# Second half of a layer norm started by single tiles, three projections in turn, and fill-in work ordered behind the chain's copies, in a hybrid RWKV-7 / short-convolution trunk layer

## The chip, the cores and the metric

The kernel runs on one core of one Trainium2 chip. The metric is the device time of one execution in microseconds (us). TensorE (PE) multiplies matrices, VectorE (DVE), ScalarE (ACT) and GpSimd (POOL) work on tiles of 128 partitions, and SyncE (SP) issues most of the DMAs. Each of the engines has its own instruction stream and works through it in order, so an instruction that waits holds up all that stand behind it on its engine.

## What is computed

One layer over 544 tokens of width 1024 (512 of a prompt, and 8 requests of 4 tokens each):

```
x    = layer_norm(ALPHA*x + 0.5*swiglu(x, ffn1), ln1)
proj = x @ w_in
r,k,v,wd,ad,gd = token-shifted mix of the first 1792 columns of proj
decay = f(w0 + tanh(wd) @ w_lora_up);  a = sigmoid(a0 + ad @ a_lora_up);  g = sigmoid(gd) @ g_lora_up
kk   = k*k_k, normalized by head;   k = k*(1 + (a-1)*k_a)
S_t  = S diag(decay) + (S (-kk)) (kk*a)^T + v k^T;   o_t = S_t r          # 8 heads of 64
y_rwkv = (group_norm(o) + sum(r*k*r_k)*v) * g
u    = c_c * c_h;   y_conv = c_b * (3-tap causal convolution of u)       # 512 channels
x    = layer_norm(ALPHA*x + [y_rwkv, y_conv] @ w_out, ln2)
x    = layer_norm(ALPHA*x + 0.5*swiglu(x, ffn2), ln3)
```

The new states (recurrence, shift, convolution) are outputs too. All numbers are fp32.

## The kernel before

**Layout.** Activations lie transposed, channels on partitions, tokens along the free axis, in two halves of the tokens (`HALF`: 256 of the prompt, then 256 and the 32 of the requests). An fp32 product is made of three matmuls: each operand is split into a high part (a copy on ACT, rounded to the type that PE multiplies) and a low part (the difference, on DVE). `mm3` issues hi·hi, hi·lo (lines 150 and 151, with the weights' high part) and lo·hi (line 152, with the weights' low part) for each 128x128 block. `split` (lines 138 and 139) does this to activations, `wsplit` (lines 134 on ACT and 135 on DVE) to weights. `wload` loads a 128x1024 block of weights by a DMA on SP into one of two `raw` buffers and splits it into one of the `hl` tiles. The next DMA into a `raw` buffer waits until both halves of its last split are done. A projection is 24 matmuls on one half of the tokens.

**Stages.** FFN1; the norm ln1 in two halves; `project` for the token-shifted columns (`project(i, mt, h, x)`: weights i, half h; 12 and 13 are the two low-rank groups, with `T12` and `sgd` as their results, 4 to 7 are k, 0 to 3 are r, 8 to 11 are v); then the recurrence for four pairs of heads. For each pair, `gates` makes the sigmoids `sw` and `a`, `square` and `norms` the norm of k, `decays` the running sums (a scan on DVE) and their exponentials, `prep` the operands of the chunks, and `scores` the chunk matrices, with copies from PSUM into BK (line 1012) and UV (line 1028) by ACT. After pairs 0 and 1, and again after 2 and 3, follow `elim` (a triangular inverse by 15 short steps on DVE, ending in the copy of line 1063), `rounds` (line 1098 on PE, line 1103 on ACT) and the chain over the chunks. The convolution's twelve projections (`conv`, and `conv_last` for its last group) and the output projection w_out (`wout`, weights `wo_0`, `wo_c`) are used as filler. Then come ln2, FFN2 and ln3.

**What sets the order.** Filler stands in a queue `bg` of generators, and `take(need)` runs them until so much PE time has been emitted. `weave(key, crit, *fill)` advances one step of the critical generator and then takes filler for its yielded need times a factor FILL[key]; `drain` empties the queue; `alt` takes its generators in turn. `tc.issue_after(ins)` places what is emitted under it behind `ins` on the same engine, and is no semaphore. From this and its own estimates a scheduler writes each engine's final order at build time. ACT's functions live in tables that have to be loaded when it goes from sigmoid to logarithm or back (lines 1380, 1381, 123: 1.28 us each).

`conv_last` loads `z` (the output of ln1 that was spilled to `xsp`, for the residual) by four DMAs, and `wout` scales each of its eight tiles by ALPHA on ACT (line 1465).

Of the kernel before, what the change touches and what calls it, by code (L numbers as in the profile page):

```python
# [61 lines left out]
def body(ctx: ExitStack, tc: tile.TileContext, xT, gu1, wd1, win, wo_c, wo_0, wo_1, gu2, wd2, wl, ln3, eye, lora, vec, cst,  # L62
# [136 lines left out]

    def weave(key, crit, *fill):  # L200
        bg.extend(fill)
        for need in crit:
            take(need * FILL[key])

    def drain(*fill):
        bg.extend(fill)
# [3 lines left out]
        for g in gens:  # L210
            yield from g

    def layer_norm(z, c0, c1, gcol, bcol, epsv, q, rs, s1, sink, table=None, hl2=None, both=False):
        n = c1 - c0
        pair = hl2 is None

# [40 lines left out]
            after(ln, tab)  # L257
        ACT.activation(rs[:, :n], rs[:, :n], AF.Exp, scale=-0.5)
        yield 1200 if pair else 600
        for d in range(0, KD, 2):  # L260
            zz = z[:, d:d + 2, c0:c1]
            DVE.tensor_tensor(zz, zz, rs[:, None, :n].to_broadcast([P, 2, n]), op=OP.mult)
# [25 lines left out]

    def to_x(spill):
        def sink(d, x, c0, c1):  # L290
            split(xhl[:, 0, d:d + 2, c0:c1], xhl[:, 1, d:d + 2, c0:c1], x)
            if spill:
                dma(xsp[:, d:d + 2, c0:c1], x)
        return sink

    def to_y(d, x, c0, c1):
# [507 lines left out]
    ln1b = layer_norm(z, *HALF[1], V_LN1G, V_LN1B, epsf, lnq, f1.lnr, f1.s1[1], to_x(True), None, f1.hl2, True)  # L804
# [36 lines left out]
    def project(i, mt, h, x):  # L841
        c0, c1 = HALF[h]
        w = wget(i)
        q = big()
        yield from mm3(q[:, :c1 - c0], w, xhl, range(KD), c0, c1)
        pb = pp.tile([P, 297], F32, name="pb", bufs=2)
        d = pp.tile([P, 288], F32, name="dt", bufs=2)
        t0 = 256 * h
        pv = pb[:, 257:297].rearrange("p (b t) -> p b t", t=5)
        if h == 0:  # L850
            POOL.memset(pb[:, 0:1], 0.0)
        else:
            POOL.tensor_copy(pb[:, 0:1], car[:, mt:mt + 1])
            POOL.tensor_copy(pv[:, :, 0], ss[:, mt, :])
        ACT.activation(pb[:, 1:257], q[:, :256], AF.Copy)
        if h:
            ACT.activation(pv[:, :, 1:5], s4(q[:, 256:288]), AF.Copy)
        ACT.activation(d[:, :c1 - c0], q[:, :c1 - c0], AF.Copy, scale=omu[:, mt:mt + 1])
        DVE.scalar_tensor_tensor(x[:, t0:t0 + 256], pb[:, 0:256], col(V_MU, mt), d[:, 0:256], op0=OP.mult, op1=OP.add)
        if h == 0:  # L860
            POOL.tensor_copy(car[:, mt:mt + 1], pb[:, 256:257])
        else:
            DVE.scalar_tensor_tensor(s4(x[:, 512:544]), pv[:, :, 0:4], col(V_MU, mt), s4(d[:, 256:288]),
                                     op0=OP.mult, op1=OP.add)
# [5 lines left out]
          project(4, 8, 0, vf))  # L870
    drain()
    dma(lo, lora)
    drain(project(0, 12, 1, T12), project(1, 13, 1, sgd), project(2, 4, 1, kf), project(3, 0, 1, rf))
    f1.close()
    zst.close()

# [32 lines left out]
    class Pair:  # L909
# [4 lines left out]
        def gates(self):  # L914
            p, fc = self.p, self.fc
            self.sw = sw = p2.tile([P, 576], F32, name="sw")
            self.a = a = p2.tile([P, 576], F32, name="a")
            qs = []
            for (t0, t1, h) in SEG:
                for r in (R(0), R(1)):  # L920
                    qs.append(sm())
                    PE.matmul(qs[-1][:, :t1 - t0], lo[r, 0, fc], T12[r, t0:t1], start=True, stop=True)
            for t0, t1, h in SEG:
                for x, q, v in ((sw, qs[2 * h], V_W0), (a, qs[2 * h + 1], V_A0)):
                    self.sg = ACT.activation(x[:, t0:t1], q[:, :t1 - t0], AF.Sigmoid, bias=col(v, p))
                    if p:
                        after(self.sg, pairs[p - 1].ke)

        def square(self, kf):
            self.kq = kq = p2.tile([P, 576], F32, name="kq")  # L930
            ACT.activation(kq, kf, AF.Square, scale=col(V_KK, self.p))

# [7 lines left out]
        def decays(self):  # L940
            p, kq = self.p, self.kq
            self.Pi = Pi = p2.tile([P, 600], F32, name="Pi")
            self.Pn = Pn = p2.tile([P, 576], F32, name="Pn")
            DVE.tensor_tensor_scan(Pn, keepm, self.sw, 0.0, op0=OP.mult, op1=OP.add)
# [33 lines left out]
        def scores(self):  # L978
# [23 lines left out]
            for a0c, n in ((0, 5), (5, 4)):  # L1002
# [300 lines left out]

    def conv_taps(i, u, us, zc):
        zs = s4(zc[:, TP:])
        for t in range(3):
# [6 lines left out]
        POOL.tensor_copy(cvo[:, i, 0:2], u[:, TP:TP + 2])  # L1313
        POOL.tensor_copy(cvo[:, i, 2:].rearrange("p (b t) -> p b t", t=2), us[:, :, 4:6])

    def conv(i):
        u = tl([P, 2 + TP + 6 * NSEQ], F32, name="cu")
# [62 lines left out]
    ACT.activation(T12[0:64, :], T12[0:64, :], AF.Tanh)  # L1380
    ACT.activation(sgd, sgd, AF.Sigmoid)
    pairs[0].gates()
    pairs[0].square(kf)
    drain(project(4, 8, 1, vf))
    pairs[0].norms()
# [53 lines left out]
    def conv_last(i=3):  # L1439
# [13 lines left out]
        conv_taps(i, u, us, zc)  # L1453
# [171 lines left out]
```

## Time and profile before

| | |
|---|---|
| three runs | 1081.84, 1085.08, 1086.4 us, median 1085.08 |
| profiled execution | 1085.56 us, its span 1083.8 us, so 1.76 us lie outside the span |
| mean granted clock of TensorE | 0.993 |
| busy: PE / DVE / ACT / POOL | 98% / 78% / 54% / 16% of the span |
| PE not busy | 27.1 us of the span |
| stages | FFN1 and ln1 to 390 us, projections and recurrence to about 700, then FFN2 |

A row of the timeline has the start in us, the duration in us, engine, line, operation, output and input with their shapes, and in brackets how long the engine had been idle before it and what released it; "x2" is two instructions in one row. A row of the windows has for each engine the busy time and the instructions in it, then the granted clock of PE (1.00 is full speed), the share of the time in which the DMA engines were busy, and what they moved. A busy PE may be one at half clock, so the clock's column is read with it.

### The profile page before, as it was taken

Reading aid. Unit: us, or ns where it says so; the run is one execution under the profiler, and the core shown is the slowest. Engines: PE = TensorE matmul, PEld = TensorE weight load, DVE = VectorE, ACT = ScalarE, POOL = GpSimd, SP = SyncE. Lnnn points to the kernel's source line nnn. Section 1 sums busy time; section 2 is a strip of 40 time slices with the busy share of each in tenths; the row PEclk is TensorE's granted clock in tenths of the full one; section 3 lists DMA queues with packets and bytes.
Section 4 is the critical chain, followed back from the end, with each engine's and each line's share of the span. In section 5 each row is a group of like instructions: output and inputs, shape, how many; then the busy total and the mean of one; then the engine's idle time right before and its main releaser. Section 6 shows DMA issues by size and latency. Waiting matters only on the chain.

```text
span 1083.8 us, 22658 instructions
## 1 busy us (share of the span) xinstructions
PE 1056.7 (98%) x9178; PEld 1014.6 (94%) x9178; DVE 841.8 (78%) x1551; ACT 582.5 (54%) x1077; POOL 177.5 (16%) x288
## 2 busy tenths in 40 slices
PE   9999999999999999999999999999999999999997
PEld 8999999999999997898879987899999999999996
DVE  7788888889775866785478657999988888888747
ACT  6655565555552667664443534667465555555523
POOL 0122220312200022142001200001312212121000
PEclk9999999999999999999999999999999999999999
DMA  8568595867854233233145723453675949678512
GB/s 283 136 125 190 120 223 127 178 155 150 189 123 146 83 109 80 65 90 79 55 146 148 192 64 126 167 155 79 141 192 120 223 109 201 148 154 186 154 42 83
DMA packets 97481, 150.00 MB, mean 138 GB/s; under 512 B 35168, under 2 KB 58592, under 8 KB 97248
## 3 DMA queue, kind: packets, MB, share of 16 engines
q1 hardware_dynamic: 70176, 112.36, 33.4%
q0 software_dynamic: 27200, 36.18, 21.9%
q8 instruction: 72, 1.18, 0.4%
q14 instruction: 33, 0.27, 0.1%
HBM read 129.86 MB, written 9.75 MB: 129 GB/s over the span
## 4 chain that ended last, share of the span: by engine, by line
PE 76%; DVE 9%; ACT 6%; issue 4%; DMA 3%; SPq 0%; POOL 0%; DVEq 0%; POOLq 0%; ACTq 0%
PE mm L530 9%; PE mm L531 8%; PE mm L532 8%; PE mm L150 7%; PE mm L151 6%; PE mm L152 6%; PE sm L532 6%; PE sm L530 6%; PE sm L531 6%; DMA raw<-in_gu 2%; ACT hl L134 2%; DVE hl L135 1%; PE sm L1098 1%; PE mm L741 1%; PE mm L705 1%
## 5 line engine op out<-in xcount | busy, mean ns | idle before, releaser
L135 DVE TENSOR_TENSOR hl<-raw,hl 128x1024 fp32r<-128x1024 f32 (+3 forms) x232 | 272.1, 1178 | 74.3 <-ACT hl L134 73.2
L134 ACT ACTIVATE hl<-raw 128x1024 fp32r<-128x1024 f32 (+3 forms) x232 | 233.2, 1019 | 86.9 <-DVE raw L497 40.0
L150 PE MATMUL mm<-xhl,hl 128*128 128x288 f32 (+1 forms) x736 | 220.1, 300 | 3.2 <-DVE z L1489 1.6
L151 PE MATMUL mm<-xhl,hl 128*128 128x288 f32 (+1 forms) x736 | 214.5, 292 | 0.3 <-DVE xhl L139 0.3
L152 PE MATMUL mm<-xhl,hl 128*128 128x288 f32 (+1 forms) x736 | 212.9, 290 | 0.1
L150 PEld LDWEIGHTS mm<-xhl,hl 128*128 128x128 f32 x736 | 139.4, 190 | 10.3 <-DVE z L1489 2.6
L151 PEld LDWEIGHTS mm<-xhl,hl 128*128 128x128 f32 x736 | 139.7, 190 | 2.7 <-issue 1.4
L152 PEld LDWEIGHTS mm<-xhl,hl 128*128 128x128 f32 x736 | 139.5, 190 | 1.2 <-issue 0.7
L532 PE MATMUL sm<-xhl,hl 128*128 128x272 f32 x432 | 125.4, 290 | 0.0
L531 PE MATMUL sm<-xhl,hl 128*128 128x272 f32 x432 | 124.5, 288 | 0.0
L530 PE MATMUL sm<-xhl,hl 128*128 128x272 f32 x432 | 124.1, 287 | 0.0
L503 POOL DMA_DIRECT2D raw<-in_gu x36 | 43.4, 1206 | 257.3 <-DVE hlb L139 155.8
L530 PE MATMUL mm<-tv,hl 128*128 128x272 f32 x288 | 83.3, 289 | 2.1 <-ACT cpb L597 1.1
L532 PE MATMUL mm<-tv,hl 128*128 128x272 f32 x288 | 83.5, 290 | 0.0
L531 PE MATMUL mm<-tv,hl 128*128 128x272 f32 x288 | 83.2, 289 | 0.0
L530 PEld LDWEIGHTS sm<-xhl,hl 128*128 128x128 f32 x432 | 81.5, 189 | 0.0
L532 PEld LDWEIGHTS sm<-xhl,hl 128*128 128x128 f32 x432 | 81.3, 188 | 0.0
L531 PEld LDWEIGHTS sm<-xhl,hl 128*128 128x128 f32 x432 | 81.3, 188 | 0.0
L509 POOL DMA_DIRECT2D raw<-in_wd x32 | 39.3, 1482 | 249.5 <-DVE hlb L139 218.7
L530 PE MATMUL mm<-hhl,hl 128*128 128x272 f32 x192 | 57.0, 302 | 0.7 <-DVE z L620 0.7
L530 PEld LDWEIGHTS mm<-tv,hl 128*128 128x128 f32 x288 | 54.3, 189 | 3.5 <-ACT cpb L591 2.1
L530 PE MATMUL sm<-hhl,hl 128*128 128x272 f32 x192 | 55.9, 291 | 0.0
(402 smaller groups left out, 2702.9 us busy)
## 6 DMA issues: line engine op xcount, KB each, us to landing
raw<-in_gu SPq DMA_DIRECT2D x84, 512.0 KB, 4.7
raw<-in_gu POOLq DMA_DIRECT2D x36, 512.0 KB, 6.2
raw<-in_wd SPq DMA_DIRECT2D x32, 512.0 KB, 4.6
raw<-in_win SPq DMA_DIRECT2D x26, 512.0 KB, 3.7
raw<-in_wd POOLq DMA_DIRECT2D x32, 256.0 KB, 7.0
z<-cpb POOLq DMA_DIRECT2D x16, 272.0 KB, 9.1
z<-sv POOLq DMA_DIRECT2D x16, 272.0 KB, 6.6
raw<-in_wo SPq DMA_DIRECT2D x8, 512.0 KB, 4.2
```

The lines of the kernel that those rows point to most:

```text
L134: ACT.activation(hl[:, 0, a:b], raw[:, a:b], AF.Copy)
L135: DVE.tensor_tensor(hl[:, 1, a:b], raw[:, a:b], hl[:, 0, a:b].bitcast(F32), op=OP.subtract)
L150: PE.matmul(out, wh, src[:, 0, k, c0:c1], start=(start and i == 0), stop=False)
L151: PE.matmul(out, wh, src[:, 1, k, c0:c1], start=False, stop=False)
L152: seen["fill"] = PE.matmul(out, wl, src[:, 0, k, c0:c1], start=False, stop=(stop and i == n - 1))
L503: POOL.dma_start(x.rearrange("p (s c) -> p s c", s=2), bass.AP(tensor=a11.tensor, offset=a11.offset, ap=[[2 * D, P], [P * 2 * D, 2], [1, 5 ...
L509: POOL.dma_start(four(x)[:, i], bass.AP(tensor=a11.tensor, offset=a11.offset, ap=[[DFF, P], [P * DFF, 2], [1, 256]]), accum_op=OP.add)
L530: PE.matmul(out, wh, src(0, i), start=(first and i == 0), stop=False, skip_group_check=True)
L531: PE.matmul(out, wh, src(1, i), start=False, stop=False, skip_group_check=True)
L532: PE.matmul(out, wl, src(0, i), start=False, stop=(i == n - 1), skip_group_check=True)
L705: seen["fill"] = PE.matmul(o[:, :n], hl[:, v, P * d:P * d + P], x[:, y, m, c0:c1], start=(first and i == 0), stop=(last and i == 2), skip_ ...
L741: seen["fill"] = PE.matmul(q[:, :n], x[:, y, m, tok], self.wm[m][:, v, c:c + n], start=False, stop=(m == n6 - 1 and i == 2), skip_group_ch ...
```

## The change

Six edits, all between the end of FFN1 and the rounds of the second group:

1. the second half of ln1 (`fine`) treats its first two of eight tiles singly, with scale and bias on DVE rather than ACT, and spills them by single DMAs; the other six stay in pairs;
2. for the second half, the projections 12, 13 and k take turns by two blocks, and r comes after them;
3. a pair's sigmoids are made in two steps: `sw` as before, `a` behind the last evacuation of k on ACT (`gates_a`);
4. the scan of `decays` is placed behind k's last mix on DVE;
5. in `weave`, filler is placed behind the last UV copy of the chunk matrices on ACT, so that filler's ACT work (the splits of line 134 among it) comes behind those copies;
6. the taps of the convolution are spread over the matmuls of its last projection, and their two copies on POOL come first.

```diff
     def weave(key, crit, *fill):
         bg.extend(fill)
+        seen["act"] = None
         for need in crit:
-            take(need * FILL[key])
+            with ExitStack() as st:
+                if seen["act"] is not None:
+                    st.enter_context(tc.issue_after(seen["act"].ins))
+                take(need * FILL[key])
...
-        for d in range(0, KD, 2):
+        for d in range(2 if fine else 0):
+            x = z[:, d, c0:c1]
+            DVE.tensor_tensor(x, x, rs[:, :n], op=OP.mult)
+            DVE.tensor_scalar(x, x, col(gcol, d), col(bcol, d), op0=OP.mult, op1=OP.add)
+            sink(d, z[:, d:d + 1, c0:c1], c0, c1)
+            yield 850
+        for d in range(2 if fine else 0, KD, 2):
...
-        ACT.activation(d[:, :c1 - c0], q[:, :c1 - c0], AF.Copy, scale=omu[:, mt:mt + 1])
+        seen["ev"] = ACT.activation(d[:, :c1 - c0], q[:, :c1 - c0], AF.Copy, scale=omu[:, mt:mt + 1])
...
-    drain(project(0, 12, 1, T12), project(1, 13, 1, sgd), project(2, 4, 1, kf), project(3, 0, 1, rf))
+    drain(alt(project(0, 12, 1, T12), project(1, 13, 1, sgd), project(2, 4, 1, kf)), project(3, 0, 1, rf))
...
+            self.sigmoids(sw, qs[0::2], V_W0)
+            self.late = partial(self.sigmoids, a, qs[1::2], V_A0)
...
+        def gates_a(self):
+            with tc.issue_after(seen["ev"].ins):
+                self.late()
...
-            DVE.tensor_tensor_scan(Pn, keepm, self.sw, 0.0, op0=OP.mult, op1=OP.add)
+            with tc.issue_after(self.mix.ins):
+                DVE.tensor_tensor_scan(Pn, keepm, self.sw, 0.0, op0=OP.mult, op1=OP.add)
...
-                    ACT.activation(UV[o, pl, par, a0c:a0c + n, :], s64(q[o, :64 * n]), AF.Copy)
+                    seen["act"] = ACT.activation(UV[o, pl, par, a0c:a0c + n, :], s64(q[o, :64 * n]), AF.Copy)
...
-        conv_taps(i, u, us, zc)
+        taps = conv_taps(i, u, us, zc)
+        next(taps)
         for h in range(2):
-            yield from conv_mm(16 + 3 * i, h, partial(conv_z, zc))
+            for n in conv_mm(16 + 3 * i, h, partial(conv_z, zc)):
+                next(taps, None)
+                yield n
...
         yield from act(pairs[p].gates)
         yield from seq(*(project(i, 4 + p, h, kf) for h in range(2)))
+        yield from act(pairs[p].gates_a)
         yield from act(pairs[p].square, kf)
```

The orders below are those of the engines' streams as built. Lines of the changed kernel differ: its lines 1033, 1049, 1124, 1493, 1475 and 1366 are lines 1012, 1028, 1103, 1465, 1448 and 1341 of the kernel before.

**First place: ACT at the beginning of the chunk matrices of pair 2.** `hl_7076` are the convolution weights of the next stage, `hl_7303` the first weights of `conv_last`. Before:

```order
L1287 ACTIVATE gq1_6717<-gq1_6717 128x288
L134 ACTIVATE hl_7076<-raw_7075 128x1024
L134 ACTIVATE hl_7303<-raw_7302 128x1024
L1012 ACTIVATE BK_4709<-sm_6824 128x320
L1012 ACTIVATE BK_4709<-sm_6825 128x320
L1028 ACTIVATE UV_4710<-sm_6838 64x320
```

and of the change:

```order
L1308 ACTIVATE gq1_6721<-gq1_6721 128x288
L1033 ACTIVATE BK_4713<-sm_6828 128x320
L1033 ACTIVATE BK_4713<-sm_6829 128x320
L1049 ACTIVATE UV_4714<-sm_6842 64x320
L1049 ACTIVATE UV_4714<-sm_6843 64x320
```

Both splits have left this place. The first (now `hl_7080`) stands behind the first UV copies of pair 3, one stage later.

**Second place: the first weights of `conv_last`, on SP and on ACT.** Before, SP has issued their DMA (`raw_7302`) two stages earlier, and behind the loads of `z` stand weights of the output projection:

```order
L1000 DMA Ad_4727<-SC_4708 64x8x64 x2
L1048 DMA AT_7146<-Ad_4727 128x16x16
L117 DMA raw_7529<-in_wo_0 128x1024
L1433 DMA y_7291<-ycd_73 128x544
L1433 DMA y_7293<-ycd_73 128x544
L1448 DMA z_7136<-xsp_72 128x1088 x4
L117 DMA raw_7534<-in_wo_c 128x1024
```

SP of the change, from the same DMA on (`raw_7306` are the first weights of `conv_last`, `raw_7351` the second):

```order
L1069 DMA AT_7150<-Ad_4731 128x16x16
L1460 DMA y_7295<-ycd_73 128x544
L1460 DMA y_7297<-ycd_73 128x544
L1475 DMA z_7140<-xsp_72 128x1088 x4
L117 DMA raw_7306<-in_win 128x1024
L117 DMA raw_7351<-in_win 128x1024
```

and ACT of the change at the split of the same weights:

```order
L134 ACTIVATE hl_7213<-raw_7212 128x1024
L1493 ACTIVATE z_7140<-z_7140 128x544 x2
L1333 ACTIVATE zc_6770<-cu_6768,vc_66 128x512
L1333 ACTIVATE zc_6770<-cu_6768,vc_66 128x32
L1493 ACTIVATE z_7140<-z_7140 128x544 x6
L134 ACTIVATE hl_7307<-raw_7306 128x1024
L134 ACTIVATE hl_7352<-raw_7351 128x1024
L1366 ACTIVATE cc_7291<-mm_7311 128x256
```

The DMA now stands behind the four loads of `z`, and the split behind the scaling of all eight tiles of `z`.

**Third place: ACT ahead of the second group's rounds**, where `hl_7530`, `hl_7535` and `hl_7790` (of the change `hl_7534`, `hl_7539`, `hl_7794`) are weights of the output projection. Before, they stand far ahead of the splits of the convolution's result (line 138):

```order
L134 ACTIVATE hl_7530<-raw_7529 128x1024
L1465 ACTIVATE z_7136<-z_7136 128x544 x2
L1341 ACTIVATE cc_7287<-mm_7307 128x256
L1341 ACTIVATE cc_7287<-mm_7378 128x288
L134 ACTIVATE hl_7535<-raw_7534 128x1024
L134 ACTIVATE hl_7790<-raw_7789 128x1024
L1310 ACTIVATE zc_7288<-cu_7286,vc_66 128x512
```

and of the change, from the last of those splits on:

```order
L138 ACTIVATE xhl_68<-zc_7292 128x288
L134 ACTIVATE hl_7534<-raw_7533 128x1024
L134 ACTIVATE hl_7539<-raw_7538 128x1024
L138 ACTIVATE xhl_68<-y_7517 128x544
L138 ACTIVATE xhl_68<-y_7519 128x544
L134 ACTIVATE hl_7794<-raw_7793 128x1024
L1124 ACTIVATE DM_4716<-sm_7550 128x512
```

All three have moved behind the split of the convolution's last result, and the third stands directly ahead of the first copy of the rounds (line 1124, before line 1103).

More of the change, by code (lines that the diff above doesn't have):

```diff
@@ L211, in seq, with layer_norm @@
             yield from g
-    def layer_norm(z, c0, c1, gcol, bcol, epsv, q, rs, s1, sink, table=None, hl2=None, both=False):
+    def layer_norm(z, c0, c1, gcol, bcol, epsv, q, rs, s1, sink, table=None, hl2=None, both=False, fine=False):
         n = c1 - c0
@@ L290, in sink @@
         def sink(d, x, c0, c1):
-            split(xhl[:, 0, d:d + 2, c0:c1], xhl[:, 1, d:d + 2, c0:c1], x)
+            w = x.shape[1]
+            split(xhl[:, 0, d:d + w, c0:c1], xhl[:, 1, d:d + w, c0:c1], x)
             if spill:
-                dma(xsp[:, d:d + 2, c0:c1], x)
+                dma(xsp[:, d:d + w, c0:c1], x)
         return sink
@@ L803, in body @@
     drain()
-    ln1b = layer_norm(z, *HALF[1], V_LN1G, V_LN1B, epsf, lnq, f1.lnr, f1.s1[1], to_x(True), None, f1.hl2, True)
+    ln1b = layer_norm(z, *HALF[1], V_LN1G, V_LN1B, epsf, lnq, f1.lnr, f1.s1[1], to_x(True), None, f1.hl2, True, True)
     ss = keep.tile([P, 14, NSEQ], F32, name="sst")
@@ L862, in project @@
         else:
-            DVE.scalar_tensor_tensor(s4(x[:, 512:544]), pv[:, :, 0:4], col(V_MU, mt), s4(d[:, 256:288]),
-                                     op0=OP.mult, op1=OP.add)
+            seen["mix"] = DVE.scalar_tensor_tensor(s4(x[:, 512:544]), pv[:, :, 0:4], col(V_MU, mt), s4(d[:, 256:288]),
+                                                   op0=OP.mult, op1=OP.add)
             POOL.tensor_copy(sho[:, mt, 0:1], pb[:, 256:257])
@@ L922, in gates, with sigmoids @@
                     PE.matmul(qs[-1][:, :t1 - t0], lo[r, 0, fc], T12[r, t0:t1], start=True, stop=True)
+            self.sigmoids(sw, qs[0::2], V_W0)
+            self.late = partial(self.sigmoids, a, qs[1::2], V_A0)
+        def sigmoids(self, x, qs, v):
+            p = self.p
             for t0, t1, h in SEG:
[L924 to L927, printed above, removed]
+                self.sg = ACT.activation(x[:, t0:t1], qs[h][:, :t1 - t0], AF.Sigmoid, bias=col(v, p))
+                if p:
+                    after(self.sg, pairs[p - 1].ke)
+        def gates_a(self):
+            with tc.issue_after(seen["ev"].ins):
+                self.late()
         def square(self, kf):
+            self.mix = seen["mix"]
             self.kq = kq = p2.tile([P, 576], F32, name="kq")
@@ L1305, in conv_taps @@
         zs = s4(zc[:, TP:])
+        POOL.tensor_copy(cvo[:, i, 0:2], u[:, TP:TP + 2])
+        POOL.tensor_copy(cvo[:, i, 2:].rearrange("p (b t) -> p b t", t=2), us[:, :, 4:6])
         for t in range(3):
@@ L1312, in conv_taps @@
                     DVE.scalar_tensor_tensor(dst, src, wt, dst, op0=OP.mult, op1=OP.add)
-        POOL.tensor_copy(cvo[:, i, 0:2], u[:, TP:TP + 2])
-        POOL.tensor_copy(cvo[:, i, 2:].rearrange("p (b t) -> p b t", t=2), us[:, :, 4:6])
+            yield 0
     def conv(i):
@@ L1382, in body @@
     pairs[0].gates()
+    pairs[0].gates_a()
     pairs[0].square(kf)
@@ L1452, in conv_last @@
             yield from conv_mm(15 + 3 * i, h, partial(conv_u, cc, u, us))
-        conv_taps(i, u, us, zc)
+        for _ in conv_taps(i, u, us, zc):
+            pass
         dma(conv_o, cvo)
```

## The prediction

> **What bounds the kernel now.** The first view is the page's head and its busy times:
>
> ```profile
> span 1083.8 us, 22658 instructions
> PE 1056.7 (98%) x9178; PEld 1014.6 (94%) x9178; DVE 841.8 (78%) x1551; ACT 582.5 (54%) x1077; POOL 177.5 (16%) x288
> ```
>
> PE is the bound, and only the 27.1 us in which it is not busy, and stretches at half clock, can be won. The change removes no matmul. So I look for where PE stands still between the end of FFN1 and the second rounds, first in the windows of 3.41 us (us, then busy time of PE, PEld, DVE, ACT, POOL, granted clock, DMA share, GB/s):
>
> ```profile
> 389.97:393.39 3.42, 1.65 (x11) 1.21 (x10) 3.42 (x7) 3.17 (x7) 0.45 (x1) 1.00 0.38 130
> 393.39:396.80 3.41, 3.41 (x17) 3.41 (x16) 3.10 (x7) 2.29 (x4) 1.21 (x3) 0.52 0.43 140
> 424.11:427.52 3.41, 1.48 (x12) 1.25 (x11) 2.48 (x5) 3.40 (x9) 1.17 (x6) 1.00 0.01 2
> 427.52:430.93 3.41, 3.41 (x11) 2.56 (x11) 1.89 (x4) 1.77 (x4) 0.59 (x3) 0.52 0.37 133
> 451.41:454.83 3.42, 2.61 (x32) 2.00 (x30) 3.42 (x8) 3.38 (x8) 0.41 (x3) 1.00 0.42 119
> 564.05:567.47 3.42, 2.42 (x33) 1.75 (x32) 1.88 (x3) 2.93 (x8) 0.00 (x0) 1.00 0.38 81
> 567.47:570.88 3.41, 3.41 (x13) 2.82 (x13) 1.28 (x3) 1.87 (x7) 0.00 (x0) 0.52 0.54 154
> ```
>
> The reader is to see three pairs of windows: one in which PE is busy for 1.65, 1.48 and 2.42 us, and behind it one in which PE is always "busy" but at clock 0.52, which does 1.7 us less work (half of 3.41). So a gap costs itself, and 1.7 us more if it makes the next window slow. Then the waits of PE, for the gap of 564:
>
> ```profile
> PE sm L1007 <- ACT BK L1012: 1.0, 1, 1.0
> PE sm L1023 <- DVE SC L996: 0.5, 2, 0.3
> ```
>
> By the clock's row, gaps of 1.0 us and a little more are enough. The Trainium skill, "TensorE: Matmul & The Clock Gate", section "What's actually happening", has the clock go cold after at least one idle window of about 3.4 us, on a free-running grid; this trace is stricter, since none of the three windows was idle. By that rule no gap of the change would be followed by a slow window unless it filled one, and the forecast below would be about 1.5 us lower.
>
> **The change part by part.** Sums are against the profiled execution (1085.56 us, span 1083.8 and 1.76 outside), which is 0.48 above the median of 1085.08.
>
> *The norm by single tiles, the projections in turn, the split sigmoids, the scan behind the mix (edits 1 to 4).* These rows carry it:
>
> ```profile
> 389.38 1.43 DVE L262 TENSOR_TENSOR z<-z,cpb 128x576 f32<-128x576 f32 x2 [0.31 <-ACT cpb L258]
> 392.09 0.53 PE L150 MATMUL mm<-xhl,hl 128*128 128x288 f32 x2 [1.51 <-ACT xhl L138]
> 399.69 0.39 ACT L855 ACTIVATE pb<-mm 128x256 f32<-128x256 f32 x1 [3.40 <-PE mm L152]
> 407.78 0.78 ACT L931 ACTIVATE kq<-k,vc 128x576 f32<-128x576 f32 x1 [0.78 <-DVE k L863]
> 415.60 0.69 ACT L952 ACTIVATE kq<-kq 128x576 f32<-128x576 f32 x1 [0.24 <-DVE kq L938]
> 422.78 0.81 DVE L976 SCALAR_TENSOR_TENSOR nk<-r,vc,k 128x576 f32<-128x576 f32 x1
> 423.51 1.35 DVE L944 TENSOR_TENSOR_SCAN Pn<-keepm,sw 128x576 f32<-128x576 f32 x1
> 425.14 0.29 PE L152 MATMUL mm<-xhl,hl 128*128 128x288 f32 x1
> 425.27 0.29 PE L150 MATMUL mm<-xhl,hl 128*128 128x288 f32 x1
> 425.67 0.24 DVE L863 SCALAR_TENSOR_TENSOR k<-pb,vc,dt 128x32 f32<-128x32 f32 x1
> 425.71 1.07 ACT L134 ACTIVATE hl<-raw 128x1024 fp32r<-128x1024 f32 x1
> 427.49 1.11 PE L937 MATMUL sm<-kq,cs 128*128 128x256 f32 x2 [1.93 <-ACT kq L931]
> ```
>
> PE waits at 392.09 for a pair of tiles; half of a pair's work should start it about a us earlier and, with three projections sharing each new pair, keep it from starving, so that the slow window of 393.39 goes. That is up to 3.5 us of PE, but it is not the path: from 399.69 to the logarithm's rows at 415.60 ACT goes almost without a break through evacuations, two table loads, sigmoids and logarithms, and waits only 0.78 and 0.24 us (rows 407.78 and 415.60). The first evacuation cannot come before the last pair's first matmuls, some 0.26 later than now, as k and 13 share PE with it. So this chain comes out 0.78 + 0.24 - 0.26 = 0.76 us earlier, and PE waits for it at pair 0's norms instead. The next meeting point is pair 1's norms at 427.49. There DVE may write k only when the products of pair 0 have read it: the last ends at 423.59, or 0.76 earlier at 422.83. The mixes are then not behind the scan (1.35) and take 425.91 - 424.78 = 1.13 us (the stretch that begins when the scan's row ends and ends with row 425.67), the square 0.78 with no weight split (1.07) ahead of it: 422.83 + 1.13 + 0.78 = 424.74 against 427.49. Of the 2.75 us, 0.92 are given back, since seven matmuls, each 0.13 after the other (425.14 and 425.27), now stand behind the norms. **Gain 1.8 us**; 0.3 if the 0.76 doesn't come and table loads fall between, 3.6 if the slow window of 427.52 goes too.
>
> *Copies ahead of filler's ACT work (edit 5), where it gains.*
>
> ```profile
> 564.49 1.06 ACT L134 ACTIVATE hl<-raw 128x1024 fp32r<-128x1024 f32 x1 [4.84 <-DMA raw<-in_win]
> 565.45 0.74 ACT L1012 ACTIVATE BK<-sm 128x320 f32<-128x320 f32 x2
> ```
>
> In pair 2's chunk matrices, ACT waits 4.84 us for weights that nobody needs yet, and the BK copies stand behind the split. With the copies first, the 1.0 us and the 0.3 beside it go, and with 1.0 us more of work in the window of 564.05 its slow successor: 1.3 + 1.7 = **3.0 us**; 1.3 if the clock stays, 3.5 at most. In pair 1's (window 451.41, 0.8 us idle) a table load and evacuations ahead of the copies go likewise: **0.8 us**, between 0 and 1.5.
>
> *Edit 5, where it loses: the weights of `conv_last`.* A split that moves behind copies keeps its `raw` buffer, so the next DMA into that buffer is issued later, and on SP it now stands behind the four loads of `z`; on ACT its split stands behind the scaling of `z`.
>
> ```profile
> 588.56 1.80 SPq L1448 DMA_DIRECT2D z<-xsp  x4
> DMA to landing us min/median/max: 6.4/8.2/9.9
> 598.50 1.21 ACT L1465 ACTIVATE z<-z 128x544 f32<-128x544 f32 x2 [0.93 <-DMA z<-xsp]
> 599.61 1.04 ACT L134 ACTIVATE hl<-raw 128x1024 fp32r<-128x1024 f32 x1
> 600.56 1.19 ACT L1465 ACTIVATE z<-z 128x544 f32<-128x544 f32 x2
> 598.27 0.28 PE L152 MATMUL mm<-xhl,hl 128*128 128x256 f32 x1
> 611.33 1.22 DVE L135 TENSOR_TENSOR hl<-raw,hl 128x1024 fp32r<-128x1024 f32 x1 [0.62 <-ACT hl L134]
> ```
>
> The landing row is that of the four loads of `z`. The last is issued at about 589.9 and, taking 9.9, lands at 599.8. Two scalings (1.2) end at 601.0, the split's high part (1.04) at 602.05, its low part on DVE (1.22, elim's last step being over by then) at 603.3. PE wants the low part at 598.27, its third matmul of this projection: 5.0 us late, and nothing else stands in PE's order at this place. Of these, PE idles about 4 us in one piece, so by the windows above a slow window follows nearly always; part of it falls into the stand, and I put it at 1.0 of its 1.7. **Loss 6.0 us.** A last landing after 6.4 us would leave 1.5; the upper end is 8.7, below.
>
> *The weights of the output projection.* Their splits now stand behind the split of the convolution's last result.
>
> ```profile
> 615.84 0.29 PE L152 MATMUL mm<-xhl,hl 128*128 128x288 f32 x1
> 616.57 0.45 DVE L1349 TENSOR_TENSOR zc<-zc,mm 128x288 f32<-128x288 f32 x1
> 617.05 0.44 ACT L138 ACTIVATE xhl<-zc 128x288 fp32r<-128x288 f32 x1 [0.83 <-DVE zc L1349]
> 617.96 0.60 ACT L1103 ACTIVATE DM<-sm 128x512 f32<-128x512 f32 x1 [0.47 <-PE sm L1098]
> raw<-in_wo_c SPq DMA_DIRECT2D x8, 512.0 KB, 3.8
> L1098 PE MATMUL sm<-DM,SC x64: 218/219/268, 616.8 to 618.6; 64*64 64x64 f32 x64
> L1098 PE MATMUL sm<-O,DM x64: 217/219/254, 619.9 to 621.8; 64*64 64x48 f32 x64
> ```
>
> Let T be the end of the last convolution matmul, 616.13. The split of its result ends at 617.49, T + 1.4. Two splits of 1.04 end at T + 2.4 and T + 3.4, so the first matmul of w_out, which follows T without a gap before, comes at T + 3.4; the low parts follow on DVE until T + 4.9. Behind the first matmuls with a low part stands the rounds' first step (616.8 before, T + 0.7), which so begins at T + 5.1. The third split needs a `raw` buffer that the low part of the first split frees at T + 3.6. Its DMA (3.8) lands at T + 7.4, its high part ends at T + 8.5, and only then may ACT copy DM for the second step of the rounds: with 0.60 for the copy at T + 9.1. In the trace this step begins at 619.9, T + 3.8. That is 5.3 later, and a slow window behind 4.5 us of idle is certain by the windows above, though mostly beside this wait: 0.5. **Loss 5.8 us**; 4.4 if the DMA is early enough that only the first delay counts, 7.5 if the slow window counts in full. The rounds are a chain, and no row shows slack behind them that would give it back.
>
> *Edit 6* reorders POOL's copies and a few DVE steps that no row of PE's waits names: nothing.
>
> Sum: -1.8 - 3.0 - 0.8 + 6.0 + 5.8 = +6.2, so 1085.56 + 6.2 = 1091.8 us. A difference under 0.5% (5.4 us) can hardly be told from no change here. The terms' bounds, not all at one end at once, give this case 1088.5 to 1095.
>
> **The rivals.**
>
> - *The weights of `conv_last` are in time* (not slower). The point is the last landing of `z`: 595.8 (598.04 for the split's end, less 1.04 and 1.2) hides all, and each us later costs one. For it: the fastest load took 6.4 us, and from 589.9 that is 596.3, a loss of 0.5. Against: row 598.50 shows ACT waiting for the third load still. Without the slow window the sum is -5.6 + 0.5 + 5.8 = +0.7: 1086.3.
> - *The DMAs behind `z` slow it.* Two blocks of 512 KB are queued right behind:
>
> ```profile
> 592.00:596.00 4.00, 4.00 (x35) 4.00 (x34) 3.86 (x12) 2.84 (x5) 0.33 (x2) 1.00 0.99 391
> ```
>
>   The DMA engines are full there (0.99), so if the queue shares them rather than serving in order, 1.05 MB at 391 GB/s come ahead of the last of `z`: 2.7 us more, 1094.5. Against: they were issued after it.
> - *The slow windows that the change removes are not in the comparison.* Their grid runs freely, and the three runs differ by 4.6 us, so other executions may lack the one at 567.47: the gain there is 1.3, and the sum +7.9: 1093.5.
> - *Both losses are hidden* because the splits wait less than I think and only the gains stay: -5.6, 1080.0. Against: the order on ACT is fixed, and the rows price each step.
>
> That the change does not do what it says is excluded for edit 5 by the orders shown, but its gain in pair 0's stage is so excluded by ACT's chain.
>
> **How the numbers follow.** Forecast 0.50, weights in time 0.17, slower `z` 0.13, windows missing 0.12, both hidden 0.08. Slower by over 0.5% means over 1090.5: of the forecast's 0.50 I give it 0.36 (its bounds reach below), of the second and third rivals 0.12 and 0.10, so 0.58. Faster is 0.07 of the last and 0.01 of the first rival, 0.08; within 0.5% the rest, 0.34. The range leaves out most of the last rival below and the far end of the slower ones above: 1083.5 to 1096.0; the forecast's own is 1088.5 to 1095.
>
> **What would show it.** Right: BK copies of pair 2 with no split ahead and no slow window at that place; PE waiting 3 to 5 us for the split of the first `conv_last` weights, with the scaling of `z` just ahead of it on ACT; PE waiting over 4 us behind the last convolution matmul, and ACT's split of a third block before the first DM copy. Wrong: if PE's waits for lines 134 and 135 at these two places sum to under 5 us, the two losses were mis-sized; if pair 1's norms still wait about 2 us with the square behind a table load, the gain of edits 3 and 4 was.

## Result: slower by 1.4%, and the profile after

| | median, us | runs | ratio to before, 95% interval |
|---|---|---|---|
| before | 1085.64 | 1081.84 to 1086.4 (4) | |
| changed | 1100.28 | 1095.97 to 1103.21 (4) | 1.0136 [1.0105, 1.0167] |

The forecast was 1091.8 with a range up to 1096.0. The direction was right and the size was not. The profiled execution of the changed kernel took 1102.87 us, 17.3 more than that of before; it is one of the longer of its four. The head of its page:

```profile
span 1101.1 us, 22659 instructions
PE 1065.4 (97%) x9178; PEld 1021.9 (93%) x9178; DVE 842.8 (77%) x1554; ACT 581.2 (53%) x1077; POOL 181.9 (17%) x288
```

PE's busy time rose by 8.7 us with the same 9178 matmuls, so part of the loss is half clock; the other half, 35.7 - 27.1 = 8.6 us, is idle time. Of PE's waits between 320 and 720 us (us in total, times, longest) four are new or have grown. Before, only the second was among them, with 1.9 us:

```profile
PE mm L150 <- ACT hl L134: 4.7, 3, 3.0
PE sm L957 <- ACT kq L951: 3.1, 2, 2.1
PE mm L152 <- DVE hl L135: 2.2, 2, 1.2
PE sm L1014 <- DVE SC L1017: 1.3, 1, 1.3
```

Lines 134 and 135 are the weights that were forecast to be late, and they are. Line 1014 (line 993 before) is the products of the chunk matrices, here those of pair 1, a place where the forecast had a gain. First the windows of the changed kernel around it and around the two places with late weights (columns as in the prediction):

```profile
447.01:450.42 3.41, 2.15 (x19) 1.84 (x19) 3.36 (x6) 0.00 (x0) 0.00 (x0) 1.00 0.31 91
450.42:453.83 3.41, 3.41 (x26) 2.95 (x25) 1.05 (x5) 1.44 (x4) 0.73 (x5) 0.52 0.51 139
453.83:457.25 3.42, 3.42 (x17) 2.85 (x16) 1.71 (x5) 0.86 (x2) 0.04 (x1) 0.50 0.41 38
457.25:460.66 3.41, 3.41 (x26) 2.36 (x25) 0.00 (x0) 1.45 (x6) 0.00 (x0) 0.50 0.00 0
460.66:464.07 3.41, 3.41 (x17) 2.99 (x17) 0.00 (x0) 0.61 (x3) 0.00 (x0) 0.50 0.02 5
...
600.61:604.02 3.41, 0.58 (x3) 0.38 (x3) 3.17 (x11) 2.60 (x3) 0.00 (x0) 1.00 0.35 63
604.02:607.43 3.41, 3.41 (x17) 3.41 (x18) 1.00 (x1) 0.00 (x0) 0.00 (x0) 0.52 0.94 151
...
624.50:627.91 3.41, 0.55 (x3) 0.34 (x3) 2.92 (x4) 2.96 (x4) 0.00 (x0) 1.00 0.49 167
627.91:631.33 3.42, 3.42 (x50) 3.20 (x52) 1.17 (x2) 0.94 (x1) 0.00 (x0) 0.52 0.76 287
```

Behind a window with PE busy 2.15 us stand four windows at half clock, not one. And a gap does not always bring one. The prediction showed the window of 564.05 of before, with PE busy 2.42 us and a slow window behind it. Five windows earlier in the same trace stands another with 2.42 us, and the next is at full clock:

```profile
546.98:550.40 3.42, 2.42 (x53) 2.08 (x48) 3.39 (x8) 1.16 (x5) 1.25 (x3) 1.00 0.40 158
550.40:553.81 3.41, 3.41 (x24) 3.17 (x23) 3.20 (x7) 0.01 (x1) 0.44 (x2) 1.00 0.58 183
```

So the length of a gap alone doesn't fix whether a slow window follows, and the prediction's reading that gaps of 1.0 us and a little more are enough does not hold even for the trace it was read from. The chunk products themselves, on the timeline of the changed kernel (24 of them, then a wait for DVE, which masks the results, then the other 10):

```profile
445.27 2.05 PE L1014 MATMUL sm<-AR,bkb 64*128 64x128 f32 x24
448.58 1.16 PE L1014 MATMUL sm<-AR,bkb 64*128 64x128 f32 x10 [1.26 <-DVE SC L1017]
```

### Where the time went, stage by stage

From here on the profiled executions are compared by how much later than before the same matmuls begin: for every matmul the start in one trace minus its start in the trace of before, the median over a stretch (in us of before), less the same at 360 to 385 us. This is worked out from the timelines, and negative is earlier. The profile of before has three slow windows of its own (393.39, 427.52, 567.47), so a step of -1.7 can mean no more than that one of them is missing. 432 lies behind pair 1's norms, 465 behind pair 1's matrices, 494 behind pair 3's norms, 575 behind pair 2's matrices (the forecast's BK copies), 604 behind the start of `conv_last`, 640 behind the start of the second rounds, 1050 behind FFN2.

```
                  432-445 465-480 494-500 545-560 575-583 604-614 640-700 1050-1070
changed             -3.6    +4.7    +5.0    +5.2    +1.8    +7.2   +12.6   +17.2
again               -2.0    +0.7    +0.7    +0.9    -2.5    +5.6   +11.7   +12.8
no5                 -3.6    +0.6    +0.5    +0.8    -1.0    -1.0    -0.4    -0.2
only5               -3.1    -3.1    -3.1    -3.1    -6.5    -1.3    +4.6    +8.9
raw3                -3.6    -0.8    -0.9    -0.7    -2.1    -0.7    -0.6    -0.9
only5_raw3          -3.0    -3.0    -3.0    -3.0    -4.6    -3.5    -3.0    -2.1
prev                -1.9    +2.2    +2.1    +2.3    +0.1    +2.7   +12.6   +15.1
only3               -1.3    +4.7    +4.7    +5.5    +5.4    +5.4    +6.1    +7.8
no35                -3.5    -3.6    +1.4    +1.7    +0.1    +0.1    +0.8    +2.6
no5_split1          -3.6    -3.6    +1.3    +1.5    -0.1    -0.1    +0.6    +2.2
no5_split1_pool     -2.0    -2.0    -2.0    -0.3    -1.7    -1.7    +2.0    +3.2
only12              -1.5    -1.5    -1.5    -1.5    -3.0    -3.0    -2.9    -0.9
prev_raw3           -3.6    -0.9    -0.9    -0.7    -3.6    -3.6    +0.0    +2.0
prev_raw3_split1    -3.5    -3.5    +1.5    +1.7    -0.9    -0.8    +3.0    +4.7
raw3_split1_pool    -2.0    -2.0    -2.0    -1.8    -2.7    -1.1    -1.0    -0.3
```

In the changed kernel five steps add up to 20.3 us: pair 1's matrices +8.3, pair 2's matrices -3.4, `conv_last` +5.4, the output projection +5.4, FFN2 +4.6. With the -3.6 ahead of them and 0.5 of small steps between they make the 17.2.

### The profile page after: what moved, and what is told of

It reads as the page before. It is cut to its first block, busy times and chain, and to the rows that moved or that the text cites. A ratio compares the mean times of both kernels' runs of the same rounds, so it can differ in the third digit from the quotient of the medians.

```text
span 1101.1 us, 22659 instructions
## 1 busy us (share of the span) xinstructions
PE 1065.4 (97%) x9178; PEld 1021.9 (93%) x9178; DVE 842.8 (77%) x1554; ACT 581.2 (53%) x1077; POOL 181.9 (17%) x288
## 4 chain that ended last, share of the span: by engine, by line
PE 38%; DVE 8%; issue 6%; ACT 4%; DMA 3%; POOL 1%; POOLq 0%; ACTq 0%; DVEq 0%
PE mm L541 4%; PE mm L150 4%; PE mm L542 4%; PE mm L543 4%; PE mm L152 3%; PE mm L151 3%; PE sm L543 2%; PE sm L541 2%; PE sm L542 2%; ACT hl L134 2%; DVE hl L135 2%; PE sm L1119 1%; DMA raw<-in_gu 1%; PE mm L752 1%; PE mm L716 1%
```

## Experiments

Each run's ratio is against the kernel before on the same chip.

**again**: the changed kernel once more.

> The changed kernel once more, for more executions and a second trace. Late weights: 11 us of lag between the matrices of pair 3 and the second rounds are in this trace too, as it depends on orders only. Cold clock: the four windows at half clock in the matrices of pair 1 (6.8 us) are in it only by chance, as two of the four runs had a mean clock of 0.992 to 0.993 and were 5 to 7 us quicker; FFN2's 4 us of lag likewise. Median 1096 to 1101 us.

1096.23 us (6 runs), 1.0100 [1.0079, 1.0121]. In its profile pair 1's matrices cost +2.7 rather than +8.3: the wait of 1.26 us is the same, but no slow window follows it, against four (4 x 1.7 = 6.8 us, of which 5.6 show as the difference). `conv_last` cost +8.1 with two slow windows behind its gap, the output projection +6.1.

**no5**: the change without edit 5.

```diff
-        seen["act"] = None
         for need in crit:
-            with ExitStack() as st:
-                if seen["act"] is not None:
-                    st.enter_context(tc.issue_after(seen["act"].ins))
-                take(need * FILL[key])
+            take(need * FILL[key])
```

> The change without edit 5 (filler is not placed behind the UV copies). Late weights: the splits stand where they stood before, the 11 us go and so do the 3 of pair 2's matrices: 1100.3 - 11 + 3 = about 1092, or less by 7 if pair 1's cold windows come with edit 5; at best edits 1 to 4 show their gain alone, 1082 to 1084. Cold clock: the stall ahead of pair 1's matrices comes from edits 1 to 4, so the cold windows stay in some runs and the time is 1089 to 1095.

1088.78 us, 1.0023 [1.0008, 1.0038]. The steps at 604 and 640 vanish (0 and +0.6). The one at pair 1's matrices stays, +4.2 with one slow window: it is not edit 5's.

**only5**: before with edit 5 alone.

> The kernel before with edit 5 alone. Late weights: +11 at the two places, -3 in pair 2's matrices, about 1093 to 1094 us. Cold clock: 1083 to 1086, since the cold windows of pair 1 and what goes with them need edits 1 to 4.

1095.07 us, 1.0084 [1.0065, 1.0102]. Both steps with weights are there, +5.2 and +5.9, and none at pair 1's matrices. Its 0.84% and no5's 0.23% make 1.07%, beside 1.00% (again) and 1.36% (the first runs) for the whole change.

**prev**: the change, with filler placed behind the last UV copy of the *previous* weave, so that no split waits for a copy of its own stage.

```diff
...
-        seen["act"] = None
+        old = seen["act"]
...
-                if seen["act"] is not None:
-                    st.enter_context(tc.issue_after(seen["act"].ins))
+                if old is not None:
+                    st.enter_context(tc.issue_after(old.ins))
```

> The change with filler placed behind the last UV copy of the pair before, without a third raw buffer. The first weights of conv_last are loaded and split ahead of z again, those of the output projection still stand behind the convolution's last result. Late weights as two separate losses: the first (5 us) goes, the second (6 us) stays, about 1096 to 1098 less 5, so 1091 to 1093. If both were one delay handed on, it would fall to 1087.

A miss: 1099.87 us, 1.0137 [1.0110, 1.0164], which fits neither of the two expected times. The step at `conv_last` shrank to +2.6 and the one at the output projection grew to +9.9. The timeline of this kernel at the first matmul of w_out, and on SP the load of the weights that it waits for:

```profile
619.52 0.80 SPq L1460 DMA_DIRECT2D y<-ycd  x2
620.37 0.90 SPq L117 DMA_DIRECT2D raw<-in_wo_c  x2
626.15 0.58 PE L150 MATMUL mm<-xhl,hl 128*128 128x256 f32 x1 [6.43 <-ACT hl L134]
```

6.43 us of waiting in one place: the load of this block now stands behind those of `y`. I read this as lateness passed on from block to block, so that the two losses are not independent; no run tests it by itself.

**raw3**: the change with a third `raw` buffer from pair 2's matrices to the second rounds.

```diff
+    rst = ExitStack()
+    wr = pool(rst, "w4r")
+    wstate["ex_raw"] = [lambda: wr.tile([P, 1024], F32, name="raw", bufs=1)]
```

> The change as it is, with a third buffer for raw weights from pair 2's matrices to the second rounds; filler still stands behind each pair's own UV copies. Late weights held up by the raw buffers: their DMAs are issued early and both splits come ahead of the two places, so the 11 us go: about 1087 to 1089. If the copies' order itself were the loss: 1096 to 1100.

1087.26 us, 1.0014 [0.9998, 1.0031]. The waits of PE for weights between 320 and 720 us are now:

```profile
PE mm L152 <- DVE hl L135: 0.6, 1, 0.6
PE mm L150 <- ACT hl L134: 0.2, 1, 0.2
```

They were 2.2 and 4.7 in the changed kernel. The first two loads of `conv_last`, which stood behind those of `z` (591.63 in the changed kernel, below), are issued some 30 us earlier:

```profile
560.27 0.33 SPq L117 DMA_DIRECT2D raw<-in_win  x1
563.71 0.38 SPq L117 DMA_DIRECT2D raw<-in_win  x1
```

Edit 5's code is kept and only the ring of `raw` buffers is longer; so it is shown that the loss comes through these buffers. With the earlier DMA the first of the two splits also stands ahead of the scaling of `z` on ACT (it starts at 586.10, against 601.09 in the changed kernel); the late DMA and the split's late place were not taken apart. The buffer isn't free: PE waits 0.60 and 0.48 us ahead of pair 2's products, and the step there is -1.4 rather than -3.4. **only5_raw3** is the same buffer on only5:

> The kernel before with edit 5 and the third raw buffer. Copies first in pair 2's matrices are worth 3 us of lag, and the late weights are gone: 1086 - 3 = about 1083. If the losses of edit 5 are not the raw buffers': 1090 or more.

1087.08 us, 1.0010 [0.9992, 1.0028] beside only5's 1.0084: the buffer takes nearly all of edit 5's loss there too, but the gain that was expected besides (1083) is not there. **prev_raw3** joins both edits:

> The change, with filler placed behind the last UV copy of the pair before instead of its own, and with a third buffer for raw weights from pair 2's matrices to the second rounds. Copies still come first in pair 2's matrices, and the weights of conv_last and of the output projection are split ahead of the two places. Late weights: the 11 us go, 1100.3 - 11 = 1089 or, without the cold windows, 1082. Cold clock alone: it stays above 1094.

1088.00 us, 1.0021 [0.9997, 1.0046], no better than raw3.

**only3**: before with the split sigmoids alone (the lines of edit 3 in the diff of the change).

> The kernel before with edit 3 alone (the sigmoids split in all pairs). Held PSUM: the stall of 1.5 us after 24 of the 34 matmuls of pair 1's matrices is there without any earlier arrival of PE, and 2 to 3 us of lag build up there: 1087.5 to 1089. If the stall needs PE to come earlier (edits 1, 2 and 4): no stall, 1085 to 1086.

1093.58 us, 1.0067 [1.0042, 1.0091]. Its step at pair 1's matrices is +6.0. PE waits there as in the changed kernel (timeline of only3):

```profile
450.98 1.16 PE L1001 MATMUL sm<-AR,bkb 64*128 64x128 f32 x10 [1.56 <-DVE SC L1004]
```

Alone, edit 3 has a cost that the whole change has not: four more ACT instructions, which are table loads. In the groups by line of only3 and then of before (count, busy us and mean ns):

```profile
L929 ACT ACT_TABLE_LOAD x5 | 6.4, 1283 | 0.1
L958 ACT ACT_TABLE_LOAD x2 | 2.6, 1283 | 0.0
```
```profile
L925 ACT ACT_TABLE_LOAD x3 | 3.8, 1283 | 0.1
```

So its 6.0 is no measure of edit 3's share.

**no35**: the change without edits 3 and 5 (besides the lines that no5 takes out, both sigmoids are made in `gates` again):

```diff
             self.late = partial(self.sigmoids, a, qs[1::2], V_A0)
+            self.late()
...
-        yield from act(pairs[p].gates_a)
...
-    pairs[0].gates_a()
```

> The change without edits 3 and 5. Held PSUM: no stall in pair 1's matrices, 1 to 2 us less than without edit 5 alone, 1086 to 1087. If edits 1, 2, 4 or 6 cost the 2 us by which the change without edit 5 is slower: 1088 to 1089.

1088.10 us, 1.0024 [1.0000, 1.0049]. The step at pair 1's matrices is gone (-3.5 to -3.6), and one of +5.0 appears at pair 3's norms, so the total is that of no5. **no5_split1** is no5 with the sigmoids of pairs 2 and 3 made in one step again, so that they stay split for pairs 0 and 1:

```diff
             self.late = partial(self.sigmoids, a, qs[1::2], V_A0)
+            if p > 1:
+                self.late()
...
-        yield from act(pairs[p].gates_a)
+        if p == 1:
+            yield from act(pairs[p].gates_a)
```

> The change without edit 5, and with the sigmoids split (edit 3) for pair 1 alone; pairs 2 and 3 make sw and a together again. Held PSUM: in the change the a sums of pair 2 keep two of the five PSUM buffers through pair 1's matrices, so PE gets through 24 of the 34 matmuls and stalls 1.5 us; here the stall and what follows it go, and the gain of 3.8 us from before it stays: 1088.8 - 3.5 = about 1085. Ahead of DVE: PE stalls because it comes to these matmuls 3.8 us earlier than DVE can mask their results; the stall stays, about 1088.8.

1089.74 us, 1.0045 [1.0027, 1.0062]: again no step at 465, +4.9 at pair 3's norms. Its timeline, first the products of pair 1 (33 of the 34 in one go), then pair 3's norms with what they wait for:

```profile
445.71 2.16 PE L1012 MATMUL sm<-AR,bkb 64*128 64x128 f32 x33
487.44 1.92 POOL L1176 COPY S<-UV 64x128 f32<-64x128 f32 x6 [11.19 <-DMA Dd<-AT]
490.68 0.19 POOL L860 COPY pb<-car 128x1 f32<-128x1 f32 x1
490.90 0.53 DVE L866 SCALAR_TENSOR_TENSOR k<-pb,vc,dt 128x256 f32<-128x256 f32 x1 [6.30 <-POOL pb L858]
491.63 0.78 ACT L949 ACTIVATE kq<-k,vc 128x576 f32<-128x576 f32 x1 [3.38 <-DVE k L870]
492.46 2.29 PE L955 MATMUL sm<-kq,cs 128*128 128x256 f32 x4 [3.30 <-ACT kq L949]
```

Read from below: PE waits 3.30 us for the square, ACT for k's mix, DVE for a shift copy on POOL (line 860; the bracket names the small one of line 858 that ends 0.03 us later), and POOL has just come through the chain's copies of S, which waited for a DMA of `elim`. **no5_split1_pool** tests this chain: the copies of S, and those that fill SI, are issued behind pair 3's shift copy.

```diff
-            POOL.tensor_copy(pb[:, 0:1], car[:, mt:mt + 1])
+            shift = POOL.tensor_copy(pb[:, 0:1], car[:, mt:mt + 1])
+            if mt == 7:
+                seen["k3"] = shift
...
+                    if g == 0 and c < 3:
+                        issue(seen["k3"], POOL.tensor_copy, Sn[R(1 - par), :, par, :], UV[R(1 - par), :, par, c + 1, :])
...
```

> The change without edit 5, sigmoids split for pair 1 alone, and POOL's copies that start the first group's chain (which wait for a DMA of elim) placed behind the shift copies of pair 3's k. A floor at pair 3's norms: the 3 us that pair 1's part keeps are lost where DVE waits for POOL's shift copy (PE idle 3.5 us, then a slow window); with the shift copy first the stall goes and the gain stays, about 1089.7 - 5 = 1085, the lag against the kernel before staying at -2.5 to -3 us. If elim and its DMAs themselves are the floor, PE waits as long at the rounds instead and the lag returns to 0 there: 1087 to 1088.

1086.78 us, 1.0004 [0.9986, 1.0022]. The step at 494 is gone. But PE then waits 2.87 us in the middle of the third step of the second rounds (before 0.28), with a slow window behind the gap, and +3.7 is given back there (timeline of this kernel):

```profile
484.88 0.19 POOL L860 COPY pb<-car 128x1 f32<-128x1 f32 x1
488.18 4.09 POOL L123 COPY S<-UV 64x128 f32<-64x128 f32 x6 [3.11 <-DMA Dd<-AT]
625.15 0.65 PE L1119 MATMUL sm<-XT,DM 64*32 64x32 f32 x22 [2.87 <-issue]
```

The new order on POOL isn't enough to cause this wait: raw3_split1_pool, which has it too, waits less than 0.2 us there and has no such step. What else causes it stays open. **raw3_split1_pool** and **prev_raw3_split1** put mends under edit 5, the second with the placement of prev and without the order on POOL:

> The change with a third raw buffer, sigmoids split for pair 1 alone, POOL's chain copies behind pair 3's shift copies. All three returns of the gains are taken away: 1087.3 - 2.5 to 3, about 1084.5 and 1 to 2 us under the kernel before. If elim is the floor: 1086 to 1087.

1087.13 us, 1.0003 [0.9985, 1.0021], over the 1084.5 that was expected.

> Filler behind the last UV copy of the pair before, a third raw buffer, and the sigmoids split for pair 1 alone. Held PSUM: 1088.0 - 3 = about 1085, with 3 us of stalls at the second rounds left. Ahead of DVE: 1088.

1091.57 us, 1.0058 [1.0034, 1.0083], a miss: it keeps the step at pair 3's norms (+5.0), and one of +3.8 at the second rounds.

**only12**: before with edits 1 and 2 alone.

> The kernel before with edits 1 and 2 alone. By the forecast's step they are not on the path: 0.8 us at most, 1085 to 1086. If PE's earlier start counts in full: 2 to 3 us of lag less at 420 us, 1083.

1086.15 us, 0.9999 [0.9979, 1.0020]: the single tiles and the projections in turn are worth nothing that can be measured. Edits 4 and 6 were not run alone. No version was found that beats before.

## Why the prediction was right in its sign and wrong in its size

**The weights of `conv_last` (+6.0): right in mechanism and sum, its parts were not.** The step is +5.4, +8.1 and +5.2 in the three profiles with edit 5 as it is. The rows of the changed kernel, from the loads of `z` to PE:

```profile
589.78 1.81 SPq L1475 DMA_DIRECT2D z<-xsp  x4
DMA to landing us min/median/max: 6.0/7.3/8.7
591.63 2.02 SPq L117 DMA_DIRECT2D raw<-in_win  x2
597.77 3.38 ACT L1493 ACTIVATE z<-z 128x544 f32<-128x544 f32 x6
601.09 1.06 ACT L134 ACTIVATE hl<-raw 128x1024 fp32r<-128x1024 f32 x1
602.20 0.39 PE L150 MATMUL mm<-xhl,hl 128*128 128x256 f32 x1 [1.61 <-ACT hl L134]
603.94 0.43 PE L152 MATMUL mm<-xhl,hl 128*128 128x256 f32 x1 [1.24 <-DVE hl L135]
```

The landing row is that of `z`. The split stands directly behind the scaling of `z`, as forecast. This alone answers the first two rivals: the weights were not in time, and `z` was hardly slowed: it landed after 6.0 to 8.7 us, in again after 6.5 to 10.7, and in before after 6.4 to 9.9. That its scaling ends at 601.15, against the forecast 601.0, is in part luck: the loads were issued 1.2 us later and landed faster. PE idled 1.61 + 1.24 us, in two pieces and under the 3 to 5 us that the prediction named as its sign and the 5.0 in its sum; the slow window behind it counted in full, 1.7 rather than 1.0. In again it was 3.69 + 0.69 us and two slow windows. The fourth rival, that both losses are hidden, falls with no5 and only5; the third applied, below.

**The weights of the output projection (+5.8): right.** The step is +5.4, +6.1 and +5.9. In the changed kernel the last convolution matmul, the first of these rows, ends at T = 623.45:

```profile
623.16 0.29 PE L152 MATMUL mm<-xhl,hl 128*128 128x288 f32 x1
624.38 1.99 ACT L134 ACTIVATE hl<-raw 128x1024 fp32r<-128x1024 f32 x2
626.42 0.39 PE L150 MATMUL mm<-xhl,hl 128*128 128x256 f32 x1 [2.96 <-ACT hl L134]
627.87 0.45 PE L152 MATMUL mm<-xhl,hl 128*128 128x256 f32 x1 [0.94 <-DVE hl L135]
630.38 1.06 ACT L134 ACTIVATE hl<-raw 128x1024 fp32r<-128x1024 f32 x1 [2.93 <-DMA raw<-in_wo_c]
631.35 0.58 ACT L1124 ACTIVATE DM<-sm 128x512 f32<-128x512 f32 x1
L1119 PE MATMUL sm<-DM,SC x64: 217/311/367, 628.9 to 631.9; 64*64 64x64 f32 x64
L1119 PE MATMUL sm<-O,DM x64: 217/219/254, 633.2 to 635.0; 64*64 64x48 f32 x64
```

First matmul of w_out at T + 3.0 (forecast 3.4), first with a low part at T + 4.4 (4.9), rounds at T + 5.4 (5.1), their second step at T + 9.7 (9.1). PE waited 2.96 + 0.94 = 3.90 us behind the last convolution matmul, just under the 4 of the prediction's sign. All waits for the weights at the two places sum to 6.75 us, over the 5 below which the losses would have been mis-sized. The two terms hang together, though: in prev the first step shrinks while the second grows.

**Pair 1's matrices (-0.8): the step that failed.** They cost +8.3, +2.7 and +4.2 in the changed kernel, again and no5. I looked only at the copies that edit 5 moves and left out what edit 3 does there. The sigmoids of the next pair (2) are made beside these matrices, and edit 3 puts those of `a` behind the last evacuation of k. On ACT before and in no5, one row of each timeline (before's reads PSUM at 449.37, no5's at 460.59):

```profile
449.37 0.54 ACT L925 ACTIVATE a<-sm,vc 128x320 f32<-128x320 f32 x1
```
```profile
460.59 0.90 ACT L936 ACTIVATE a<-sm,vc 128x256 f32<-128x256 f32 x2
```

The products that fill these sums begin at 445.90 in before and at 442.06 in no5. So two sums of `a` hold two of the five PSUM buffers named sm for some 19 us rather than 4; the chunk products use these buffers too, and PE stops after 24 of these 34 products until DVE's mask has freed one. Taking the split away (no35, or for pairs 2 and 3 alone, no5_split1) takes away the wait of 1.26 us and the step, so the split is shown to be its cause. That the held buffers are the link follows from the order and the buffers; a kernel with more of them wasn't tried. The wait is short; what made it dear in the changed kernel are the four slow windows behind it: without them, in again, the step was 5.6 us smaller. Nor is the total shorter without the split: the lead that is kept at pair 1 is lost at pair 3's norms, and no35 (1.0024) and no5_split1 (1.0045) are no faster than no5 (1.0023).

**Edits 1 to 4 (-1.8): no gain to speak of.** At 432 to 445 all kernels are 1.3 to 3.6 us ahead, only5 too (-3.1), though it lacks these edits. Its profile has neither of the two slow windows of before (393.39 and 427.52), and nor has that of the changed kernel (-3.6); what the edits add is the difference, 0.5. So the lead is the rival that I had priced for pair 2's matrices alone: slow windows that other executions may not have. It is luck that pair 1's norms begin at 424.75, as forecast (424.74): the matmuls there lead those of before by 3.0 us, and 1.5 of it is there in only5 too, without the edits. (The 1.13 us of the mixes in that sum is counted from 424.78, where the scan's row ends at 424.86; this is 0.08 us.) The sign I had named for it is there as well; the square of pair 1's norms still stands behind a table load, and PE waits 2.10 us for it, where before it waited 1.93:

```profile
422.06 1.28 ACT L123 ACT_TABLE_LOAD   x1
423.93 0.77 ACT L951 ACTIVATE kq<-k,vc 128x576 f32<-128x576 f32 x1 [0.58 <-DVE k L874]
424.75 1.24 PE L957 MATMUL sm<-kq,cs 128*128 128x256 f32 x4 [2.10 <-ACT kq L951]
```

only12's ratio of 0.9999 agrees.

**Pair 2's matrices (-3.0): half of it.** The changed kernel gains 3.4 there, again 3.4, only5 3.4, and the BK copies come with no split ahead. But no5, which leaves the splits ahead of the BK copies, gains 1.8 by missing the slow window at 567.47. So some 1.6 us are edit 5's, near the 1.3 of the third rival, and the other 1.8 are again a slow window that other executions may not have.

With -0.5 for edits 1 to 4 (-3.6 against only5's -3.1), -1.6, and pair 1's matrices at again's +2.7, the forecast's sum becomes -0.5 - 1.6 + 2.7 + 6.0 + 5.8 = 12.4 rather than 6.2. The ratios 1.0100 and 1.0136 are 10.9 and 14.8 us. So the two losses were about right, and the three gains, -5.6 in the forecast, came to +0.6; of this difference of 6.2 us, 3.5 are the step at pair 1's matrices.

**What stays open.** FFN2 adds +4.6 (changed), +1.1 (again), +4.3 (only5) and about 0 (no5, raw3), with code that no edit touches. Waits for copies, 1.9 and 1.2 us, and a slow window at 1006.8 make it up in the changed kernel; whether a shifted start or chance decides, no run tells. Nor was it tried why pair 3's norms don't wait for POOL's copies in before. There r's matmuls stand ahead of the norms and may cover them, which is only argued.

## What to carry to other kernels

Order that puts a split behind a copy also delays the next DMA into that split's buffer: follow the ring of buffers to the DMA's new place in its queue, and cost the buffer that would take the wait away (here it removed nearly all of edit 5's loss). An evacuation that is moved later holds its PSUM buffer for that long, so ask who else takes buffers from that pool meanwhile. Before a gain is booked for a half-clock window that goes, look whether other executions, or edits elsewhere, lose it too.

## What the runs showed of the hardware

A gap can cost much more than the 1.7 us of one slow window. Behind the window of 447.01, with PE busy 2.15 of 3.41 us, the clock stayed at half for four windows, 13.65 us; in again the same place, behind a window with PE busy 2.18 us, had none. And equal gaps differ within one trace: of the two windows of before with PE busy 2.42 us, the one of 564.05 is followed by clock 0.52, the one of 546.98 by 1.00. The Trainium skill, "TensorE: Matmul & The Clock Gate", "What's actually happening", has the clock go cold after at least one idle window, on a free-running grid. The slow windows of the changed kernel that begin at 450.42, 604.02 and 627.91 fit a grid: they lie 45 and 7 steps of 3.413 us apart, each with 0.52. The condition does not fit, since none of the windows ahead of them was idle, and here the measurement decides. What makes one such window cold and not the other, these runs don't show.
